# Expert weights of a two-layer mixture: down weights unsplit, the others split by two engines, more load buffers

## The chip, the cores and the metric

The kernel runs on one core of a Trainium2 chip. The core has five engines with their own instruction streams: TensorE (PE, matrix products), VectorE (DVE), ScalarE (ACT), GpSimd (POOL) and SyncE (SP), whose queue issues most of the transfers from DRAM. The metric is the device time in microseconds (us); lower is better. Before the change it is 4615.15 us, the median of three runs (4608.68 to 4620.15).

## The reference, cut to what matters

A first block (differential attention, two gated linear recurrences, an MLP) is followed by two layers. Each layer adds a mixer's output and then a mixture of 16 experts, on 1024 tokens of width 1024, all in float32:

```python
def ec_moe(h, w_router, w_gate, w_up, w_down):
    cap = EC_FACTOR * s // N_EXPERTS                       # 128 tokens an expert
    logits = jnp.einsum('bsd,de->bse', h, w_router)
    aff = jax.nn.softmax(logits, axis=-1)
    gates, idx = lax.top_k(aff.transpose(0, 2, 1), cap)    # each expert takes its own tokens
    xs = jax.vmap(lambda hb, ib: hb[ib])(h, idx)
    g = jnp.einsum('becd,edf->becf', xs, w_gate)           # 1024 -> 512
    u = jnp.einsum('becd,edf->becf', xs, w_up)             # 1024 -> 512
    y = jnp.einsum('becf,efd->becd', jax.nn.silu(g) * u, w_down)   # 512 -> 1024
    y = y * gates[..., None]
    return scatter_add(idx, y)
```

An expert's three matrices have 2 MB each, so a layer reads 16 x 6 MB of expert weights.

## The kernel before, in words

Products of float32 numbers are formed from float32r parts. `split_into` (L98, L99) makes `hi`, the number rounded to float32r by ScalarE, and `lo`, the rest, by a subtraction on VectorE or GpSimd. `mm3` (L91 to L93) then adds three products: hi x hi, hi x lo and lo x hi. A weight chunk of [128, 1024] numbers, 512 KB, is loaded by `whalf` (L114) from SP's queue into a raw buffer and split into a `whi` and a `wlo` buffer; `lo_engine` gives every other subtraction to GpSimd and to VectorE.

A layer's second half is `out_moe`. It first runs the mixer's output projection over eight token tiles (its matrix stands split on chip, in the pool `eT` or `ow`), with the norm and the router's logits of each tile (`moe_in`). While this goes on, the first raw buffers of the pool `mx` are freed one after the other by small GpSimd copies, so that expert weights come in. Then `moe` runs:

- `top_c` finds every expert's 128 best tokens in 15 rounds of comparisons on VectorE and one small product each (L1491);
- `route(e)` builds a one-hot table (L1542), reads out token numbers and gates by small products, and gathers the tokens' rows with an indirect transfer of GpSimd (L1553);
- `tokens` transposes the gathered rows and splits them into `xe`;
- `up(e, ...)` multiplies them with the gate and then the up matrix, four chunks each, into the PSUM tile `pgu`;
- `hidden` takes Silu (L1581) and the product with the up part (L1582), transposes that (L1586) and splits it into `se`;
- `down` multiplies with the four chunks of the down matrix into `pd`;
- `add` scales the result by the gate (L1604) and adds it to the rows in DRAM with an indirect transfer of GpSimd (L1605).

The program's order interleaves experts: the gate and up products of expert e, then the down products of expert e-1. A planner with a cost model sets the final order of each engine's stream from the program's order and the buffers. All twelve chunks of an expert are split, through 18 raw buffers (`mx`) and 8 pairs of hi/lo buffers in the space of the projection's matrix. The first eight chunks of a layer are subtracted by GpSimd alone, while VectorE is at the selection. In layer 1, the last one, `finish` norms the output rows beside the last experts, and gathers, adds and norms the rows of experts 14 and 15 once more at the end (L1980, L1985).

Of the kernel before, what the change touches and what calls it, by code (L numbers as in the profile page):

```python
# [26 lines left out]
class Kern:  # L27
# [6 lines left out]
    # ---------------------------------------------------------------- consts  # L34
# [20 lines left out]
    def exp_ln_table(self):  # L55
        """Exp and Ln from the one table set that holds both."""
        from concourse.act_sets import SETS
        i = [t.name for t in SETS].index("natural_log_exp_and_others")
        self.tc.keep_in_program_order(self.nc.scalar.add_instruction(mybir.InstLoadActFuncSet(
            name=self.nc.get_next_instruction_name(), act_func_set_id=i, ins=[], outs=[])))  # L60

    # ---------------------------------------------------------------- psum
# [3 lines left out]
    def mb(self, name="mb"):  # L66
        """A single bank: the even layer has four of them in place of two pairs."""
# [4 lines left out]
    def pair(self):  # L72
        """Two banks."""
        if self.pss:
            return [self.mb(), self.mb()]
        p = self.mm()
        return [p[:, 0, :], p[:, 1, :]]
# [10 lines left out]
    # ---------------------------------------------------------------- helpers  # L88
# [6 lines left out]
    def split_into(self, src, hi, lo, leng=None):  # L95
        """hi = src rounded to float32r, lo = src - hi, both exact parts of src."""
# [9 lines left out]
    def whalf(self, *srcs, W=None):  # L106
        """Pieces of weights, each [128, n, m], side by side in one 1024-wide chunk (hi, lo)."""
# [13 lines left out]
    def parts(self, w, m, off=0, n=None):  # L121
        """The (hi, lo) pieces of width m of a chunk."""
# [3 lines left out]
    def wsrc(self, w, r0, nk, c0, m):  # L126
        """[128, nk, m] view of the DRAM matrix w: rows r0 + 128 k + p, columns c0..c0+m."""
# [3 lines left out]
    def w128(self, w, c0, W=None):  # L131
        """128 columns of a matrix with 1024 rows: 8 pieces [128, 128]."""
        return self.parts(self.whalf(self.wsrc(w, 0, 8, c0, 128), W=W), 128)

    def w256(self, w, c0, W=None):
        """256 columns of a matrix with 1024 rows: 8 pieces [128, 256]."""
# [5 lines left out]
    def row(self, src, n, name, pool, bufs=None, off=0):  # L142
        """A DRAM vector repeated on every partition."""
# [5 lines left out]
    def colrow(self, cols, out, n):  # L149
        """Columns [128, n] to a row of 128 n values on every partition: out [128, n*128]."""  # L150
# [9 lines left out]
    def rstd(self, ss, n, out):  # L160
        """out = (ss / n + eps) ** -0.5 on a narrow tile."""
# [10 lines left out]
    def ssq(self, xt, out, s):  # L172
        """Sum of squares along the free axis; s: scratch."""
        self.nc.scalar.activation(s, xt, AF.Square, accum_out=out)

    def norm_tile(self, xt, g, pool, xb=2):
        """rms norm of a token tile [128, 1024] with gain row g."""
# [8 lines left out]
    def rstd_dve(self, ss, n, out):  # L186
        """out = (ss / n + eps) ** -0.5 on the vector engine alone: a guess from the bits, three Newton steps."""
# [16 lines left out]
    def norm_tiles(self, xs, g, xn, keep=None):  # L204
        """xn = rms norms of token tiles [128, 1024] with gain row g; rows times keep."""
# [10 lines left out]
    def cols_T(self, xs, hT, t0, g, sh, pool, by_class=False):  # L216
        """Token tiles xs (each [128, 1024]) transposed, times the gain columns g, plus the columns sh,
        into hT (hi, lo) [128, 8, 1024] from token tile t0 on; by_class: token 4 j + c of a tile at
        place 32 c + j."""
# [29 lines left out]
    def norm_T(self, xin, g, hT, sp):  # L249
        """rms norm of the token tiles in DRAM, gain row g, into hT (hi, lo) [128, 8, 1024]."""  # L250
# [11 lines left out]
    def proj_T(self, wl, hT, out, h, k0=0):  # L262
        """out [128 columns, 512 tokens] of half h."""
# [3 lines left out]
    def proj_T2(self, wl, hT, k0=0):  # L267
        """[128 columns, 1024 tokens] in psum."""
# [5 lines left out]
    def proj_N(self, wl, hT, t, out, k0=0):  # L274
        """out [128 tokens of tile t, columns]."""
# [3 lines left out]
    def proj_N2(self, wl, hT, evac, ps, k0=0):  # L279
        """256 columns for all tokens; evac(t2, psum [128, 2 token tiles, 256])."""  # L280
# [6 lines left out]
    # ---------------------------------------------------------------- small vectors and modulation  # L287
    def condition(self, pool):
        """Silu of c, as columns."""
# [9 lines left out]
    def vectors(self, pool):  # L299
        """Small vectors as columns: loaded as rows of 128, transposed at once."""  # L300
# [24 lines left out]
    def ada_sums(self, s, pool, tag, bufs, acc=None):  # L325
        """Section s of the modulation but for its bias, still to be summed over the partitions; acc: what is there."""
# [13 lines left out]
    def ada(self, s, pool, tag, bufs, ps):  # L340
        """Section s of the modulation, as columns mod[:, 8 s : 8 s + 8]."""
# [7 lines left out]
    def mod_cols(self, name, s_sh, s_sc, nm):  # L349
        """Columns g * (1 + scale) and shift for one modulated norm."""  # L350
# [5 lines left out]
    # ---------------------------------------------------------------- attention pieces  # L356
    def q_stack(self, src, pb, dst, scale=1.0):
        """src [64, n] psum at partition pb -> dst [128, n]: float32r head and rest stacked."""
# [6 lines left out]
    def k_stack(self, src, pb, kh, kl, both=True):  # L365
        """src [64, n] psum at partition pb -> kh, kl [128, n]: each part on both halves."""
# [8 lines left out]
    def scores(self, out, q, kh, kl, t):  # L375
        """out [128, 2, 512] = q tile t against all keys, from stacked parts."""
# [8 lines left out]
    def pt_tiles(self, sp, nb):  # L385
        """Transposed weights of two query tiles: [half of the keys][hi, lo] tiles [128 k, 4, 256]."""
# [3 lines left out]
    def p_transpose(self, e, pt, qi, sp=None):  # L390
        """e [128 q, 1024] into pt at query tile qi of the pair; the second half by way of sp and GpSimd."""
# [14 lines left out]
    # ---------------------------------------------------------------- differential attention  # L406
    def branch_a(self, hT, oa, first):
        nc, tc, a = self.nc, self.tc, self.a
        W = a["w_in"]
        with ExitStack() as ctx:  # L410
            sp = ctx.enter_context(tc.tile_pool(name="da", bufs=1))
            self.exp_ln_table()
            # lambda
# [15 lines left out]
            # distances times the head's slope, a quarter of it for the next head  # L429
# [23 lines left out]
    def diff_head(self, sp, Q, KK, V, tab, nlam, ones, gcol, oa, h):  # L453
        nc = self.nc
        for qr in range(4):
            pt = self.pt_tiles(sp, 2)
            rc = sp.tile([128, 2], F32, name="drc", tag="drc", bufs=2)
            for qi in range(2):
# [13 lines left out]
                # (e1 - lam s1 / s2 e2), divided by s1 at the end  # L472
# [22 lines left out]
    def rstd_wide(self, ss, n, out):  # L495
        """out = (ss / n + eps) ** -0.5 over a wide tile."""
# [4 lines left out]
    # ---------------------------------------------------------------- gated linear recurrences  # L501
# [18 lines left out]
    def softplus_neg_abs(self, z, sp, bias=None):  # L520
        """Ln(1 + exp(-|z + bias|))."""
# [1597 lines left out]
```

## Time and profile before

| what | value |
|---|---|
| runs | 4615.15 us median, 4608.68 to 4620.15 (three) |
| profiled execution, first to last instruction | 4606.6 us |
| median run less that span | 8.5 us |
| TensorE busy | 4061.6 us (88%) |
| VectorE, ScalarE, GpSimd busy | 2627.1 (57%), 1967.3 (43%), 1696.7 us (37%) |
| transfers | 514.39 MB, mean 112 GB/s |
| mean granted TensorE clock | 0.917 |

The profiled execution has no time of its own beside its span; the runs' median stands 8.5 us above it. A group's line gives count, busy time, mean duration in ns, the idle time of the engine just before, and what ended that. A timeline's line gives start, duration, engine, source line, operation, output and input, and in brackets an idle time with its releaser. A wait's line gives the total, the count and the longest. TensorE's records overlap, so the time between two starts is what a product costs, not a record's duration.

### The profile page before, as it was taken

The page shows a single profiled execution, that of the slowest core. Times are in us where ns is not written, and L with a number is a line of the kernel's source. Part 1 is how long each engine was busy: PE and PEld are TensorE (multiplying, and loading weights), DVE is VectorE, ACT ScalarE, POOL GpSimd, SP SyncE. Part 2 cuts the span into 40 slices and gives each one's busy share as a digit, 9 for nine tenths or more (in the row PEclk, how much of TensorE's full clock was granted, in tenths as well). Part 3 has the DMA queues.
Part 4 walks back from the last instruction along what each step waited for, and adds up shares of the span by engine and source line. Part 5 has one row for each costly group of instructions (what it writes and reads, how often), then busy time and mean ns, then how long its engine had stood idle before and what let it go on. Part 6 is the DMA issues. An engine that isn't in the chain of part 4 may idle for free. (4 is left out here: it accounts for less than half of the span.)

```text
span 4606.6 us, 57724 instructions
## 1 busy us (share of the span) xinstructions
PE 4061.6 (88%) x21893; PEld 3397.3 (74%) x21893; DVE 2627.1 (57%) x3944; ACT 1967.3 (43%) x3192; POOL 1696.7 (37%) x1082
## 2 busy tenths in 40 slices
PE   6999989899899999998999987778796899986786
PEld 5788867778587888887889866666694787865564
DVE  6545573636434333336255565978638567648886
ACT  3444333432323112114354542556524578734564
POOL 2000031231333212125211222777424467616775
PEclk8999989686999999998989998889897999997898
DMA  4212341021432111122322226788510001066886
GB/s 158 74 49 81 101 132 47 33 84 43 159 119 73 51 42 55 42 60 91 86 72 77 66 74 233 238 278 295 152 43 9 16 19 47 19 224 216 299 292 217
DMA packets 346937, 514.39 MB, mean 112 GB/s; under 512 B 39318, under 2 KB 212769, under 8 KB 346660
## 3 DMA queue, kind: packets, MB, share of 16 engines
q1 hardware_dynamic: 337012, 475.58, 31.8%
q0 software_dynamic: 9648, 35.13, 3.1%
q8 instruction: 172, 2.82, 0.3%
q14 instruction: 105, 0.86, 0.1%
HBM read 418.87 MB, written 83.36 MB: 109 GB/s over the span
## 5 line engine op out<-in xcount | busy, mean ns | idle before, releaser
L99 POOL TENSOR_TENSOR wlo<-wraw,whi 128x1024 fp32r<-128x1024 f32 (+2 forms) x297 | 775.0, 2696 | 1371.9 <-ACT whi L98 1318.2
L98 ACT ACTIVATE whi<-wraw 128x1024 fp32r<-128x1024 f32 (+2 forms) x579 | 597.2, 1041 | 922.4 <-PE mm L92 259.7
L99 DVE TENSOR_TENSOR wlo<-wraw,whi 128x1024 fp32r<-128x1024 f32 (+3 forms) x282 | 651.4, 2323 | 545.7 <-ACT whi L98 513.2
L91 PE MATMUL mm<-h,whi 128*128 128x512 f32 x832 | 331.6, 400 | 8.0 <-DVE xq L649 4.2
L92 PE MATMUL mm<-h,whi 128*128 128x512 f32 x832 | 331.5, 398 | 2.9 <-POOL h L99 1.8
L93 PE MATMUL mm<-h,wlo 128*128 128x512 f32 x832 | 331.5, 399 | 1.4 <-POOL wlo L99 1.1
L91 PE MATMUL pgu<-whi,xe 128*128 128x512 f32 x512 | 216.2, 422 | 10.9 <-ACT xe L98 10.8
L93 PE MATMUL pgu<-whi,xe 128*128 128x512 f32 x512 | 215.9, 422 | 0.0
L912 DVE TENSOR_TENSOR Y<-py,Y 128x1024 f32<-128x1024 f32 x112 | 137.0, 1224 | 133.3 <-PE py L93 133.3
L92 PE MATMUL pgu<-wlo,xe 128*128 128x512 f32 x512 | 212.0, 414 | 0.0
L91 PE MATMUL py<-whi,mr 128*128 128x512 f32 x512 | 201.6, 394 | 9.2 <-DVE mr L921 8.1
L93 PE MATMUL py<-whi,mr 128*128 128x512 f32 x512 | 203.1, 397 | 0.0
L92 PE MATMUL py<-wlo,mr 128*128 128x512 f32 x512 | 202.3, 395 | 0.0
L1023 DVE TENSOR_REDUCE ast<-ps 128x1 f32<-128x1024 f32 x128 | 156.3, 1222 | 66.3 <-PE ps L93 47.6
L91 PEld LDWEIGHTS mm<-h,whi 128*128 128x128 f32 x832 | 156.8, 189 | 47.7 <-issue 5.3
L396 PE MATMUL ptp<-ident,e 128*128 128x128 f32 x1280 | 181.1, 276 | 12.0 <-ACT pf L400 5.1
L92 PEld LDWEIGHTS mm<-h,whi 128*128 128x128 f32 x832 | 157.3, 189 | 41.5 <-POOL h L99 2.3
L93 PEld LDWEIGHTS mm<-h,wlo 128*128 128x128 f32 x832 | 157.2, 189 | 40.6 <-POOL wlo L99 2.0
L91 PE MATMUL pj<-h,whi 128*128 128x512 f32 x384 | 159.7, 416 | 19.1 <-ACT gst L791 18.9
L402 POOL TENSOR_TENSOR pt<-pf,pt 128x512 fp32r<-128x512 f32 x128 | 165.8, 1295 | 10.6
L396 PEld LDWEIGHTS ptp<-ident,e 128*128 128x128 f32 x1280 | 148.3, 142 | 27.2 <-ACT pf L400 11.4
L92 PE MATMUL pd<-wlo,se 128*128 128x512 f32 x256 | 113.4, 443 | 51.6 <-DVE wlo L99 51.6
(636 smaller groups left out, 11488.7 us busy)
## 6 DMA issues: line engine op xcount, KB each, us to landing
wraw<-in_moe_w_gate_dram SPq DMA_DIRECT2D x128, 512.0 KB
wraw<-in_moe_w_up_dram SPq DMA_DIRECT2D x128, 512.0 KB
wraw<-in_moe_w_down_dram SPq DMA_DIRECT2D x128, 512.0 KB
wraw<-in_mlp_w_dram SPq DMA_DIRECT2D x64, 512.0 KB
wraw<-in_w_in_dram SPq DMA_DIRECT2D x52, 512.0 KB
wad<-in_ada_w_dram SPq DMA_DIRECT2D x48, 512.0 KB
gD<-gst SPq DMA_DIRECT2D x24, 512.0 KB
wraw<-x SPq DMA_DIRECT2D x20, 512.0 KB
```

Source lines behind the costliest of these rows:

```text
L91: t.matmul(out, l[0], r[0], start=start, stop=False)
L92: t.matmul(out, l[0], r[1], start=False, stop=False)
L93: return t.matmul(out, l[1], r[0], start=False, stop=stop)
L98: nc.scalar.activation(hi, src, AF.Copy)
L99: (nc.gpsimd if leng == "pool" else nc.vector).tensor_tensor(lo, src, hi.bitcast(F32), op=ALU.subtract)
L396: nc.tensor.transpose(p[:, k, :], e[:, (4 * kg + k) * 128:(4 * kg + k + 1) * 128], self.ident)
L402: nc.gpsimd.tensor_tensor(lo, f, hi.bitcast(F32), op=ALU.subtract)
L912: nc.vector.tensor_tensor(y, pv, y, op=ALU.add)
L1023: nc.vector.tensor_reduce(out=st[:, 0:1], in_=pv, axis=AX.X, op=ALU.min)
```

## The change

It touches the mixtures alone. The pieces, with what is not needed left out:

```diff
+        n = [0]
+        def raw(nm, chunk):
+            pool, bufs = (W[0], W[1]) if n[0] % (W[1] + W[3]) < W[1] else (W[2], W[3])
+            n[0] += 1
+            x = pool.tile([128, 1024], F32, name="wraw", tag="wraw", bufs=bufs)
+            nc.sync.dma_start(x, dap(a[nm], chunk * 128 * 1024, [[1024, 128], [1, 1024]]))
+            return x
+
+        def weights(nm, chunk):
+            x = raw(nm, chunk)
+            hi, lo = [W[2].tile([128, 1024], FR, name=y, tag=y, bufs=W[4]) for y in ("whi", "wlo")]
+            self.split_into(x, hi, lo)
+            return self.parts((hi, lo), 512)
...
-            sT = [sp.tile([128, 4, 128], FR, name="se%d" % j, tag="se%d" % j, bufs=2) for j in range(2)]
+            sT = sp.tile([128, 4, 128], F32, name="se", tag="se", bufs=2)
...
-            self.split_into(p, sT[0], sT[1])
+            nc.scalar.activation(sT, p, AF.Copy)
...
-                w = weights("moe_w_down_2", ((i * 16 + e) * 512 + k * 128) * 1024, [[1024, 128], [1, 1], [1, 1024]])
+                w = raw("moe_w_down_2", (i * 16 + e) * 4 + k)
                 for h in range(2):
-                    self.mm3(p[:, h, :], (sT[0][:, k, :], sT[1][:, k, :]), w[h], k == 0, k == 3)
+                    nc.tensor.matmul(p[:, h, :], sT[:, k, :], w[:, h * 512:(h + 1) * 512], start=k == 0, stop=k == 3)
...
-        slot = self.top_c(lg, sr, cs, begun)
+        slot = self.top_c(lg, sr, cs)
...
-        self.moe(i, xD, hD, lg, opn("mo"), sr, cs, (mx, 18, 8, hl), finish)
+        cls(hl)
+        mw = opn("mw", "left" if side == "right" else "right")
+        self.moe(i, xD, hD, lg, opn("mo", side), sr, cs, (mx, 18, mw, 8, 4), finish)
+        cls("mo", "mr", "mx", "mw")
...
+    for n in ("moe_w_gate_2", "moe_w_up_2"):
+        w = np.asarray(inputs[n]).reshape(2 * 16 * 4, 2, 128, 512)
+        data[n] = np.ascontiguousarray(w.transpose(0, 2, 1, 3))
```

- Down weights and hidden values stay whole: one plain float32 product takes the place of three float32r ones, straight from the raw buffer.
- Gate and up chunks are still split, `hi` by ScalarE and `lo` always by VectorE. GpSimd's part, and the function `begun` that started it, are gone.
- The pool of the projection's matrix is closed and a pool `mw` takes its place, with 8 more raw buffers and 4 pairs in place of 8. Chunks go through the 18 and the 8 raw buffers in turn.
- Gate and up weights are laid out anew before the launch, so that a chunk's two row blocks stand side by side: a partition reads 4 KB in one piece in place of two pieces of 2 KB.
- In layer 1 the pools of `out_moe` lie on the other side of the on-chip memory, where the attention's tiles were.

Comments and function descriptions are taken out as well.

More of the change, by code (lines that the diff above doesn't have):

```diff
@@ L1465, in route_consts, with top_c @@
         return r
-    def top_c(self, aff, sp, cs, begun):
+    def top_c(self, aff, sp, cs):
         nc = self.nc
@@ L1482, in top_c @@
         nc.vector.tensor_copy(ah, at.bitcast(BF)[:, 1::2])
-        begun(at[:, 0:1])
         msk = [ta("msk%d" % i, [128], BF) for i in range(3)]
@@ L1534, in moe @@
                 nc.gpsimd.tensor_tensor(rest[k + 1], rest[k], val[:, :, :, k], op=ALU.subtract)
-        def begun(x):
-            for _ in range(W[2]):
-                nc.gpsimd.tensor_copy(W[3].tile([128, 1024], FR, name="whi", tag="whi", bufs=W[2])[:, 0:1], x)
-        slot = self.top_c(lg, sr, cs, begun)
+        slot = self.top_c(lg, sr, cs)
         def route(e):
@@ L1554, in route @@
             return off, gate, xg
-        def weights(nm, off, dims):
-            self.nw += 1
-            self.lo_engines = ("pool", "dve") if self.nw > W[2] else ("pool",)
-            return self.parts(self.whalf(dap(a[nm], off, dims), W=W), 512)
-        self.nw = 0
+        n = [0]
[10 more added lines that the diff above has]
+            return self.parts((hi, lo), 512)
         def tokens(xg):
@@ L1573, in up @@
             for kg in range(4):
-                wl = weights(nm, ((i * 16 + e) * 1024 + kg * 256) * 512, [[512, 128], [512 * 128, 2], [1, 512]])
+                wl = weights(nm, (i * 16 + e) * 4 + kg)
                 for k in range(2):
@@ L1934, in last @@
             hl = opn("eT", "right")
-            T.extend((self.w_rows("even_w_out_2", hl), hl))
+            T.extend((self.w_rows("even_w_out_2", hl), "eT"))
         self.even_attn(h, a["even_w_in_2"], eD, s1, W2, between, last)
         cls("eb", "ea")
-        self.out_moe(0, *T, eD, 5, x2, x3, h4, opn, cls, banks, None)
-        cls("mo", "mr", "mx", "eT")
+        self.out_moe(0, *T, eD, 5, x2, x3, h4, opn, cls, banks, None, "left")
         dd = opn("dd", "right").tile([128, NT, 768], F32, name="dd")
@@ L1985, in finish @@
                 nc.gpsimd.indirect_dma_start(out=out, out_offset=r[e][0], in_=xn, in_offset=None)
-        self.out_moe(1, wl, hl, cD, 7, x3, x5, h6, opn, cls, banks, finish)
-        cls("mo", "mr", "mx")
-        cls("ow")
+        self.out_moe(1, wl, "ow", cD, 7, x3, x5, h6, opn, cls, banks, finish, "right")
         cls("ps")
@@ L1995, in w_rows, with out_moe @@
                 for k in range(8)]
-    def out_moe(self, i, wl, hl, src, late, xin, xD, hD, opn, cls, banks, finish):
+    def out_moe(self, i, wl, hl, src, late, xin, xD, hD, opn, cls, banks, finish, side):
         nc = self.nc
-        mx = opn("mx")
-        sr = opn("mr")
+        mx = opn("mx", side)
+        sr = opn("mr", side)
         lg = sr.tile([128, NT, 16], F32, name="lg")
         cs = self.route_consts(sr)
-        sp = opn("eo")
+        sp = opn("eo", side)
         half, whole = self.moe_in(i, sp, hD, lg)
```

## The prediction

> **What bounds the kernel now.** I read the page's slices first, then the stages, the groups and waits in them, and single instructions last. A slice is 4606.6 / 40 = 115 us; the two expert mixtures are slices 26 to 29 and 37 to 40.
>
> ```profile
> PE   6999989899899999998999987778796899986786
> POOL 2000031231333212125211222777424467616775
> ```
>
> TensorE is near 9 almost everywhere, but falls to 6 to 8 in the mixtures, just where GpSimd rises. The stages, in the view by window (between the first and the last Silu of a mixture):
>
> ```profile
> core 0: us, PE busy (x) PEld busy (x) DVE busy (x) ACT busy (x) POOL busy (x), PEclk, DMA share, GB/s
> 2915.00:3283.00 368.00, 301.31 (x1319) 238.13 (x1318) 306.34 (x181) 229.61 (x251) 289.31 (x115) 0.90 0.83 274
> 4196.00:4570.00 374.00, 304.16 (x1338) 239.88 (x1336) 314.06 (x196) 233.75 (x260) 288.41 (x114) 0.91 0.82 278
> ```
>
> TensorE idles there for some 70 us a layer, and its granted clock is 0.90. The Silu of an expert (L1581) and the scaling of its share (L1604) mark the experts, in the timeline of ScalarE:
>
> ```profile
> 2915.76 0.60 ACT L1581 ACTIVATE es<-pgu 128x512 f32<-128x512 f32 x1
> 2935.42 1.13 ACT L1604 ACTIVATE whi<-pd,gate 128x1024 f32<-128x1024 f32 x1 [0.28 <-PE pd L93]
> 2953.53 1.12 ACT L1604 ACTIVATE whi<-pd,gate 128x1024 f32<-128x1024 f32 x1 [0.29 <-PE pd L93]
> 3282.32 0.60 ACT L1581 ACTIVATE es<-pgu 128x512 f32<-128x512 f32 x1 [0.28 <-PE pgu L93]
> 4196.49 0.60 ACT L1581 ACTIVATE es<-pgu 128x512 f32<-128x512 f32 x1
> 4570.01 0.58 ACT L1581 ACTIVATE es<-pgu 128x512 f32<-128x512 f32 x1
> ```
>
> Fifteen steps take 366.6 and 373.5 us: 24.4 and 24.9 us an expert. One step, 2935.4 to 2953.5, took 18.1 us: there the split weights were ready and TensorE alone set the pace. So about 6.5 us a step are waits. For what, the groups, two waits and the timeline say:
>
> ```profile
> L99 DVE TENSOR_TENSOR wlo<-wraw,whi 128x1024 fp32r<-128x1024 f32 x97 | 268.9, 2791 | 81.3 <-ACT whi L98 77.5 <-DMA wraw<-in_moe_w_gate_dram 3.8
> L99 POOL TENSOR_TENSOR wlo<-wraw,whi 128x1024 fp32r<-128x1024 f32 x97 | 266.3, 2873 | 70.7 <-ACT whi L98 70.5
> L98 ACT ACTIVATE whi<-wraw 128x1024 fp32r<-128x1024 f32 x194 | 204.0, 1062 | 105.9 <-PE pd L93 46.1 <-PE pgu L93 44.4 <-issue 5.3
> L99 DVE TENSOR_TENSOR wlo<-wraw,whi x282: 410/1272/13774, 30.1 to 4578.9; 128x1024 fp32r<-128x1024 f32 x137, 128x768 fp32r<-128x768 f32 x2, 128x256 fp32r<-128x256 f32 x1, 128x384 fp32r<-128x384 f32 x1
> 3083.77 6.69 POOL L99 TENSOR_TENSOR wlo<-wraw,whi 128x1024 fp32r<-128x1024 f32 x2
> 3084.84 3.41 DVE L99 TENSOR_TENSOR wlo<-wraw,whi 128x1024 fp32r<-128x1024 f32 x1
> 3090.61 1.78 POOL L1553 DMA_INDIRECT wraw<-h,idx  x1 [0.15 <-issue]
> 3091.47 1.21 DVE L99 TENSOR_TENSOR wlo<-wraw,whi 128x1024 fp32r<-128x1024 f32 x1
> PE pd L92 <- DVE wlo L99: 25.8, 5, 5.8
> PE pse L1586 <- DVE xe L99: 19.4, 7, 5.0
> SPq L114 <- POOL wlo L99: 151.7, 46, 32.9
> SPq L114 <- DVE wlo L99: 133.1, 60, 13.8
> ```
>
> The subtraction (L99) takes VectorE 1.21 us when GpSimd runs none, 3.41 us beside one, and up to 13.8 us; its mean here is 2.79. The two engines hinder each other, six chunks each cost both some 17 us a step, and TensorE and the weight loads' queue wait behind them. The bound of the mixtures is the splitting.
>
> **The change, part by part.** Per expert, twelve chunks of 512 KB.
>
> Removed: four of twelve splits, so four L98 (4 x 1.06 us of ScalarE) and four L99. GpSimd keeps its two indirect transfers only. Hidden values need one copy (L98) and no L99.
>
> Moved: the eight remaining L99 all go to VectorE. The price is bounded by 1.21 us (alone) and 2.79 (mean beside GpSimd); I take 1.22, since GpSimd has no tensor work left and the 1.21 us row ran beside an indirect transfer. VectorE also has the one-hot table `oh`, the pieces of `xe`, and the product `es`, whose shape is that of `xe`:
>
> ```profile
> L1542 DVE TENSOR_TENSOR oh<-one_to,slot 128x1024 bf16<-128x1024 bf16 x9 | 22.4, 2487 | 5.3 <-PE pj L1546 5.3
> L99 DVE TENSOR_TENSOR xe<-pxe,xe 128x512 fp32r<-128x512 f32 x26 | 16.8, 676 | 0.0
> ```
>
> Sum: 8 x 1.22 + 2 x 0.68 + 0.68 + at most 2.49 + 0.3 (gate, index) = 14.6 us a step. ScalarE: 8 x 1.06 + three pieces of 0.6, Silu 0.6, L1604 1.1 = 12. Both lie under TensorE.
>
> Added: a float32 product in place of three float32r ones. The trace has none in the mixture; the nearest is the gMLP's, two products in four records, beside the cadence of gate and up:
>
> ```profile
> 2240.59 1.98 PE L1151 MATMUL pm<-z,zwt 128*128 128x512 f32 x4 [0.20 <-DVE zwt L1143]
> L1151 PE MATMUL pm<-z,zwt x8: 592/592/697, 2240.6 to 2245.1; 128*128 128x512 f32 x8
> 4200.17 0.39 PE L91 MATMUL pgu<-whi,xe 128*128 128x512 f32 x1
> 4200.41 0.39 PE L92 MATMUL pgu<-wlo,xe 128*128 128x512 f32 x1
> ```
>
> A float32 record starts every (1.98 - 0.59) / 3 = 0.463 us, so a product is 0.926 us; three float32r are 3 x 0.233 = 0.70. Eight products a step (four chunks, two halves): 8 x (0.926 - 0.70) = +1.8 us on TensorE. Its step becomes 18.1 + 1.8 = 19.9. So TensorE's work grows; it gains only by not waiting.
>
> Buffers: 26 raw in place of 18, hi/lo pairs 4 in place of 8. A pair is in use for 6 x 0.233 = 1.4 us; refilling takes about 0.35 + 1.06 + 0.15 + 1.22 + 0.15 = 2.9 (durations above; the gaps are an estimate from the 0.28 in the L1604 row). Four pairs turn round in 5.6 us, against 4.3, so the loop holds, with 1.3 us of slack for VectorE's other pieces. During the 7.4 us of down products four chunks get ready. What the slack does not take I put at 0.6 us a step (0 to 2, the latter when `oh` and an `xe` fall among the splits). **Step: 20.5 us.** Behind a delayed L98, ScalarE's queue holds the next L98, Silu and `xe`, for which TensorE would wait.
>
> Loads: gate and up rows grow from 2 KB to 4 KB a partition. The rates, first two stretches with mostly 2 KB rows and then 4 KB alone, and two crowded ones in the mixture; and what a mixture moves:
>
> ```profile
> 2832.00:2836.00 4.00, 4.00 (x18) 3.20 (x18) 1.72 (x9) 1.13 (x4) 0.00 (x0) 1.00 1.05 390
> 4560.00:4564.00 4.00, 4.00 (x19) 3.23 (x18) 1.34 (x2) 3.79 (x8) 0.00 (x0) 1.00 1.03 419
> 3180.00:3200.00 20.00, 15.75 (x69) 11.95 (x68) 14.93 (x11) 11.52 (x13) 17.52 (x7) 0.83 1.02 352
> 3200.00:3220.00 20.00, 15.49 (x70) 12.32 (x69) 17.11 (x11) 13.10 (x15) 17.88 (x7) 0.97 0.92 302
> q0 software_dynamic: 4188, 15.23, 16.2%
> ```
>
> Some 28 of 192 chunks are there when the mixture starts, so 164 x 0.524 + 15.2 (indirect) = 101 MB have to come in about 320 us: 316 GB/s. The chip gave 352 under full load with the short rows; I expect about 370 and no wait. That is a margin of a sixth, not more.
>
> Selection of the tokens: the small product of a round (L1491) waited 2.57 us for VectorE beside GpSimd's splits, and 1.40 after them:
>
> ```profile
> 2861.77 0.19 PE L1491 MATMUL po<-cnt,same_expert 128*128 128x4 bf16 x1 [2.57 <-DVE msk L1488]
> 2877.50 0.19 PE L1491 MATMUL po<-cnt,same_expert 128*128 128x4 bf16 x1 [1.40 <-DVE msk L1488]
> ```
>
> Eight slow rounds cost 8 x 1.2 = 9 us more than fast ones; against it stand four first L99 now queued in VectorE among the rounds, 4 x 1.22 = 4.9 us. I take a gain of 3 us a layer (a loss of 3 to a gain of 8).
>
> The pools' sides: in layer 1 the raw buffers now lie where the attention's tiles were, so their first loads, and the router's small ones ahead of them in SP's queue, wait for its end. But SP issues them late already:
>
> ```profile
> 4103.54 2.48 SPq L114 DMA_DIRECT2D wraw<-in_moe_w_gate_dram  x4
> ```
>
> That is 93 us before that layer's first Silu (4196.5), and the output projection covers it: 18 chunks are 9.4 MB, 24 us at 390 GB/s. I put it at nothing; without that cover it would be these 24 us. The eight further buffers open once that projection has read its matrix, and fill during the selection, as eight freed ones did before.
>
> Sum, layer 0: from the first Silu to the end of the last down product (3295.7) 379.9 us now; then 15 x 20.5 + 7.4 (the last down product) + 1.3 (the wait for its hidden values, an estimate) = 316: -64. Layer 1: 373.5 to 307.5: -66; its end hangs on the indirect transfers, not on the splits. The last down product of layer 0, and in layer 1 the scaling of share 13 and the addition of share 15:
>
> ```profile
> 3295.30 0.40 PE L93 MATMUL pd<-whi,se 128*128 128x512 f32 x1
> 4543.38 1.12 ACT L1604 ACTIVATE whi<-pd,gate 128x1024 f32<-128x1024 f32 x1 [0.28 <-PE pd L93]
> 4589.90 1.28 DVE L1980 SCALAR_TENSOR_TENSOR wraw<-pd,gate,wraw 128x1024 f32<-128x1024 f32 x1 [3.56 <-DMA wraw<-x,idx]
> ```
>
> From share 13 to share 15 are 46.5 us now, with a step of some 26 in it; the chain of scatter, eight loads, scatter and gather does not shrink with the step, so I give back 2. Selection: -6. Total -64 - 64 - 6 = -134 us: a span of 4473. The runs' median, 4615.15, is 8.5 us above the profiled span; I keep that: **4481 us**.
>
> **The rivals.** Loads bind. If they only reach 302 GB/s, 101 MB take 335 us, 15 more a layer: 4511; at the mean of the stage, 276, 366 us: 4571. Against it: that mean has the queue waiting 285 us for buffers. Chance 0.10.
>
> Four pairs are too few. A step with 2 us more (22.5) gives 4481 + 2 x 15 x 2 = 4541. For it: ScalarE already waits 46.1 and 44.4 us for TensorE to free pairs, with eight. 0.15.
>
> VectorE becomes the bound, the slower side: were L99 2.79 us even without GpSimd, eight and the rest make 27.1 us a step, 4481 + 30 x 6.6 = 4679. It decides from 8d + 4.8 = 24.7, so d = 2.5 us. The rows of 1.21 and 3.41 speak against it. 0.05. The Trainium skill, SBUF — State Buffer, "Who interferes with whom", has a VectorE instruction with two SBUF inputs fully blocked by a GpSimd one that reads SBUF, and not slowed otherwise. By that rule the price falls back to the 1.21 of the row and the time is the forecast; by the mean it is this rival. The row of 13.8 us agrees with the rule.
>
> Float32 is dearer: four records of 0.463 a product make 12.5 + 14.8 + 0.6 = 27.9 us a step, 4703. Against it: L1151 shows eight records for four products. 0.04. The Trainium skill, FP8 and Floating Point Precision, "TensorE Precision Notes", counts four passes for true float32, which speaks against this edit. Were each pass a record, it would be this rival; by the two records of L1151 a record holds two passes, and the forecast stands.
>
> The change does not act, since another limit keeps the step at 24.7: 4615. The 18.1 us step speaks against it. 0.03.
>
> **How the numbers follow.** The forecast has 0.63, with its own range of 4450 to 4515 (steps of 19.9 to 21.5, selection's bounds). The range 4440 to 4570 takes in the loads and the pairs, and leaves out 0.12 and a little at the low end. No change means within 0.3%, about what runs of this kernel can tell. Faster 0.63 + 0.10 + 0.15 = 0.88, same 0.03, slower 0.09.
>
> **What would show it.** Right: Silus 20 to 21 us apart; VectorE's L99 at 1.2 us; two float32 records a down product, 0.46 us apart; clock near 1.0 in the mixtures; TensorE's waits on L99 gone. Wrong: L99 over 2 us, records over 0.6 us apart, ScalarE or TensorE waiting on each other's pairs for more than 2 us a step, or down products waiting for raw chunks.

## The result, and the profile after

The changed kernel takes 4461.01 us, the median of four runs (4452.69 to 4473.79); the kernel before, beside it, 4617.65 us (4608.68 to 4620.29). The ratio is 0.9669 with a 95% interval of 0.9645 to 0.9693: 156.6 us less. The forecast was 4481 us, 20 us too high.

The profiled run of after took 4473.79 us with a span of 4472.0, so only 1.8 us lie outside the span. The profiled run of before, with a span of 4606.6, was therefore the fastest of its runs (4608.68), and the profiled run of after is the slowest of its four. The spans differ by 134.6 us, the medians by 156.6. Both differences are used below.

The slices of the page of after, with its two groups of interest (columns of a group: busy us, mean ns, idle time before and its releaser):

```profile
PE   6999989989889999998999998699895988996997
POOL 2000021322153212124411121111123646630111
PEclk8999989886899999999998998799996999997998
L99 DVE TENSOR_TENSOR wlo<-wraw,whi 128x1024 fp32r<-128x1024 f32 (+1 forms) x354 | 441.9, 1251 | 632.0 <-ACT whi L98 604.1
L1600 PE MATMUL pd<-wraw,se 128*128 128x512 f32 x512 | 236.6, 596 | 1.9 <-ACT se L1592 1.9
```

In the mixtures (now slices 27 to 29 and 37 to 40) GpSimd has fallen to about 1 and TensorE is at 9 in the slices that lie wholly in a mixture (28, 38 and 39). From the first to the last Silu of each mixture, by window (PE, PEld, DVE, ACT and POOL busy, then granted clock, DMA share, GB/s), and the groups of layer 0's:

```profile
2920.71:3217.72 297.01, 292.65 (x1213) 198.97 (x1212) 182.26 (x193) 168.72 (x189) 39.79 (x26) 1.00 0.93 330
4134.79:4437.09 302.30, 294.32 (x1216) 199.09 (x1214) 187.68 (x210) 177.24 (x204) 41.59 (x27) 1.00 0.93 335
```
```profile
L99 DVE TENSOR_TENSOR wlo<-wraw,whi 128x1024 fp32r<-128x1024 f32 x118 | 144.3, 1225 | 86.5 <-ACT whi L98 85.0 <-DMA wraw<-in_moe_w_gate_dram 0.2 <-DMA wraw<-in_moe_w_down_dram 0.2
L98 ACT ACTIVATE whi<-wraw 128x1024 fp32r<-128x1024 f32 x117 | 123.8, 1061 | 87.5 <-PE pgu L93 87.4
```

TensorE is busy in 98.5% of the first window, at full granted clock (before: 82% and 0.90). The subtraction takes 1.225 us. The arrow has turned: before, TensorE waited for the subtraction; now ScalarE's copies (L98) wait 87.4 us for TensorE to free a pair. TensorE sets the pace. The timeline of ScalarE has the first and last Silu (L1586) of both layers, and scalings of shares (L1609) in layer 0:

```profile
2920.71 0.60 ACT L1586 ACTIVATE es<-pgu 128x512 f32<-128x512 f32 x1
...
2958.43 1.12 ACT L1609 ACTIVATE whi<-pd,gate 128x1024 f32<-128x1024 f32 x1 [1.89 <-PE pd L1600]
2978.03 1.11 ACT L1609 ACTIVATE whi<-pd,gate 128x1024 f32<-128x1024 f32 x1 [1.03 <-PE pd L1600]
...
3157.44 1.12 ACT L1609 ACTIVATE whi<-pd,gate 128x1024 f32<-128x1024 f32 x1 [0.18 <-PE pd L1600]
3178.10 1.12 ACT L1609 ACTIVATE whi<-pd,gate 128x1024 f32<-128x1024 f32 x1 [0.17 <-PE pd L1600]
...
3217.72 0.60 ACT L1586 ACTIVATE es<-pgu 128x512 f32<-128x512 f32 x1 [9.68 <-PE pgu L93]
...
4134.79 0.60 ACT L1586 ACTIVATE es<-pgu 128x512 f32<-128x512 f32 x1
...
4437.09 0.58 ACT L1586 ACTIVATE es<-pgu 128x512 f32<-128x512 f32 x1
```

Fifteen steps take 297.0 and 302.3 us: 19.8 and 20.15 us an expert, in place of 24.4 and 24.9. The first of the fifteen intervals holds only a part of a step (14.9 us), so a whole step is a little longer than the mean. Early steps are mostly 19.6 us, late ones 20.7. In the early ones TensorE shows no idle time. From the tenth step on it stands still at the change of expert, for the token pieces `xe` or for another small piece, 0.53 or 0.82 us in each late step. Two early steps by window, from Silu to Silu, and the first of the waits in TensorE's timeline:

```profile
3035.15:3074.36 39.21, 39.21 (x169) 26.95 (x168) 25.44 (x28) 23.25 (x26) 5.84 (x3) 1.00 1.02 369
```
```profile
3096.47 0.50 PE L91 MATMUL pgu<-whi,xe 128*128 128x512 f32 x1 [0.58 <-ACT xe L98]
```

**The account of the spans.** Each stretch runs from a first record to a last one in both traces. "Projection" is the output projection of a layer's second half.

| stretch | before | after | difference |
|---|---|---|---|
| start to the first router product of layer 0 (L1441) | 2760.7 | 2771.5 | +10.8 |
| from there to the end of layer 0's last down product | 535.0 | 456.7 | -78.3 |
| to the last projection product of layer 1 | 834.0 | 842.3 | +8.3 |
| to the first Silu of layer 1 | 66.8 | 64.3 | -2.5 |
| to the end | 410.1 | 337.2 | -72.9 |
| sum | 4606.6 | 4472.0 | -134.6 |

The first and third rows are work that the change doesn't touch; TensorE's instructions of the first are the same in the same order in both kernels. At 2628 us the two traces stand level; by 2706 us after is 10.5 us behind. The profile shows what differs there: in layer 0's attention the granted clock (the figure before the DMA share) was 0.99 in the run of before and 0.84 in that of after. The first line is of before, the second of after:

```profile
2620.00:2710.00 90.00, 86.13 (x478) 69.81 (x478) 70.74 (x204) 65.17 (x173) 25.11 (x18) 0.99 0.33 97
```
```profile
2620.00:2710.00 90.00, 87.06 (x426) 69.76 (x425) 64.42 (x178) 58.11 (x151) 22.66 (x17) 0.84 0.28 85
```

In the same 90 us TensorE got through 478 products in one run and 426 in the other. Without these 19.1 us the spans would differ by 153.7 us, close to the medians. The third row is settled less well: its clock was lower only in part, but two kernels below that keep the pools as before took 840.0 and 843.5 us for it, so the moved pools don't explain it.

**The selection.** Last product of the projection in layer 0, first and last round; first before, then after, which also shows the first four splits:

```profile
2846.57 0.40 PE L93 MATMUL mb<-whi,wlo 128*128 128x512 f32 x1
2854.91 0.16 PE L1491 MATMUL po<-cnt,same_expert 128*128 128x4 bf16 x1 [1.72 <-DVE msk L1488]
...
2885.43 0.19 PE L1491 MATMUL po<-cnt,same_expert 128*128 128x4 bf16 x1 [1.40 <-DVE msk L1488]
```
```profile
2857.28 0.40 PE L93 MATMUL mb<-whi,wlo 128*128 128x512 f32 x1
2857.71 3.91 ACT L98 ACTIVATE whi<-wraw 128x1024 fp32r<-128x1024 f32 x4 [2.21 <-PE mb L93]
2858.81 4.63 DVE L99 TENSOR_TENSOR wlo<-wraw,whi 128x1024 fp32r<-128x1024 f32 x4 [0.40 <-ACT whi L98]
2869.57 0.16 PE L1490 MATMUL po<-cnt,same_expert 128*128 128x4 bf16 x1 [1.71 <-DVE msk L1487]
...
2891.75 0.19 PE L1490 MATMUL po<-cnt,same_expert 128*128 128x4 bf16 x1 [1.40 <-DVE msk L1487]
```

The rounds shrink from 30.5 to 22.2 us, since no GpSimd subtraction runs beside them. But the first round now comes 12.3 us after the projection, not 8.3: the four first splits stand on ScalarE and VectorE ahead of the last token tile's norm.

### The profile page after: what moved, and what is told of

It reads as the page before. It is cut to its first block, busy times and chain, and to the rows that moved or that the text cites. A ratio compares the mean times of both kernels' runs of the same rounds, so it can differ in the third digit from the quotient of the medians.

```text
span 4472.0 us, 56648 instructions
## 1 busy us (share of the span) xinstructions
PE 4064.7 (91%) x21637; PEld 3331.6 (74%) x21637; DVE 2365.1 (53%) x3984; ACT 1839.8 (41%) x3064; POOL 1140.9 (26%) x866
## 3 DMA queue, kind: packets, MB, share of 16 engines
q8 instruction: 170, 2.79, 0.3%
## 5 line engine op out<-in xcount | busy, mean ns | idle before, releaser
L98 ACT ACTIVATE whi<-wraw 128x1024 fp32r<-128x1024 f32 (+3 forms) x451 | 465.3, 1035 | 926.5 <-PE mm L92 260.9
L99 DVE TENSOR_TENSOR wlo<-wraw,whi 128x1024 fp32r<-128x1024 f32 (+1 forms) x354 | 441.9, 1251 | 632.0 <-ACT whi L98 604.1
L99 POOL TENSOR_TENSOR wlo<-wraw,whi 128x1024 fp32r<-128x1024 f32 (+3 forms) x97 | 229.0, 2361 | 1269.7 <-ACT whi L98 1244.3
L1600 PE MATMUL pd<-wraw,se 128*128 128x512 f32 x512 | 236.6, 596 | 1.9 <-ACT se L1592 1.9
L91 PE MATMUL pgu<-whi,xe 128*128 128x512 f32 x512 | 216.7, 424 | 5.2 <-ACT xe L98 5.2
L93 PE MATMUL pgu<-whi,xe 128*128 128x512 f32 x512 | 204.7, 400 | 0.0
L91 PE MATMUL pj<-h,whi 128*128 128x512 f32 x384 | 159.3, 415 | 16.8 <-ACT gst L791 16.6
```

What stands on the lines that cost most here:

```text
L91: t.matmul(out, l[0], r[0], start=start, stop=False)
L93: return t.matmul(out, l[1], r[0], start=False, stop=stop)
L98: nc.scalar.activation(hi, src, AF.Copy)
L99: (nc.gpsimd if leng == "pool" else nc.vector).tensor_tensor(lo, src, hi.bitcast(F32), op=ALU.subtract)
L1600: nc.tensor.matmul(p[:, h, :], sT[:, k, :], w[:, h * 512:(h + 1) * 512], start=k == 0, stop=k == 3)
```

## The experiments

The theory at this point: the mixture was held by two engines that slow each other, and TensorE takes over once the subtractions run on VectorE alone. The main rival: only the number of splits matters, whoever does them. "Step" is the mean distance of the Silus in layer 0 and layer 1.

| kernel | median us | ratio to before, 95% interval | steps, us |
|---|---|---|---|
| changed | 4461.0 | 0.9669 (0.9645 to 0.9693) | 19.8, 20.15 |
| 1: changed, GpSimd back | 4514.7 | 0.9777 (0.9749 to 0.9805) | 20.85, 21.1 |
| 2: before, VectorE alone | 4484.8 | 0.9726 (0.9698 to 0.9754) | 20.1, 20.25 |
| 3: changed, down weights split | 4475.7 | 0.9688 (0.9661 to 0.9716) | 19.7, 20.1 |
| 4: changed, 2 KB rows | 4466.9 | 0.9660 (0.9637 to 0.9683) | 19.8, 20.2 |
| 5: before, float32 down products | 4481.2 | 0.9700 (0.9672 to 0.9728) | 19.8, 20.5 |
| 6: changed, 18 raw and 8 pairs | 4475.4 | 0.9690 (0.9673 to 0.9708) | 19.6, 20.3 |
| 7: changed, half of the down products | 4435.9 | 0.9612 (0.9586 to 0.9637) | 19.1, 19.0 |
| 8: changed, two of four down chunks split | 4464.1 | 0.9659 (0.9639 to 0.9679) | 19.3, 20.0 |
| 9: run 6 with GpSimd back | 4486.9 | 0.9723 (0.9708 to 0.9738) | 19.7, 20.3 |
| 10: changed, three pairs | 4454.7 | 0.9655 (0.9640 to 0.9670) | 19.7, 20.0 |
| 11: changed, pairs open early | 4459.7 | 0.9668 (0.9654 to 0.9681) | 19.8, 19.95 |
| 12: runs 8 and 11 together | 4447.2 | 0.9636 (0.9623 to 0.9649) | 19.4, 19.7 |

### Which part brought the gain (runs 1, 2, 3 and 5)

**Run 1, GpSimd back.**

```diff
-            self.split_into(x, hi, lo)
+            self.split_into(x, hi, lo, leng=("pool", "dve")[n[0] % 2])
```

> The changed kernel, but every other subtraction of the gate and up weights goes to GpSimd again (4 of 8 an expert). Theory A, the two engines hinder each other: VectorE's 128x1024 L99 goes back from 1.23 us to a mean above 2 us, and with four pairs a chunk takes 1.4 + 0.35 + 1.06 + 0.15 + 2.8 + 0.15 = 5.9 us to turn round, 1.48 us a chunk against the 1.40 that TensorE needs; the step grows from 19.8 to 21 to 22.5 us, 4500 to 4540 us in all. Theory B, the gain came from splitting 8 chunks in place of 12, whoever does it: step 19.8, 4461 within 12 us, since 4 x 2.8 us on either engine lie far under the step.

Measured: 4514.7 us, 54 more than the changed kernel, steps of 20.85 and 21.1 us. The groups of its first mixture:

```profile
L99 POOL TENSOR_TENSOR wlo<-wraw,whi 128x1024 fp32r<-128x1024 f32 x60 | 152.0, 2555 | 95.8 <-ACT whi L98 95.8
L98 ACT ACTIVATE whi<-wraw 128x1024 fp32r<-128x1024 f32 x117 | 123.9, 1060 | 113.7 <-PE pgu L93 104.5 <-issue 9.2
L99 DVE TENSOR_TENSOR wlo<-wraw,whi 128x1024 fp32r<-128x1024 f32 x59 | 116.2, 1975 | 108.8 <-ACT whi L98 108.8
```

VectorE's subtraction is back at 1.98 us on average and GpSimd's takes 2.56. The time is that of theory A, the mean and the step fall just short of it. TensorE's waits in that mixture are 12.1 us for `es`, which stands in VectorE's queue behind a slowed subtraction, and 4.0 us for subtractions themselves. The Trainium skill, SBUF — State Buffer, "Who interferes with whom", says that the two engines contend only where they share a port; these means, and the 1.225 us once GpSimd has no subtraction, agree.

**Run 2, the kernel before with VectorE alone** from a layer's ninth chunk on, and twelve splits an expert:

```diff
-            self.lo_engines = ("pool", "dve") if self.nw > W[2] else ("pool",)
+            self.lo_engines = ("dve",) if self.nw > W[2] else ("pool",)
```

> The kernel before, with all twelve splits and three float32r products a down product, but from the ninth chunk of a layer on every subtraction goes to VectorE. Theory A: GpSimd's part is the whole trouble. VectorE then has 12 x 1.22 + 3 x 0.68 + 0.68 + 2.5 + 0.3 = 20.2 us a step, TensorE 18.1: step 20.2 to 21 in place of 24.7, 4480 to 4505 us, nearly all of the change's gain without the plain float32 products. Theory B: VectorE cannot carry twelve; the fewer splits are needed: step 23 or more, 4565 or more.

Measured: 4484.8 us, 132.6 less than before, the time of theory A. The window of its first mixture:

```profile
2909.26:3210.46 301.20, 280.94 (x1313) 223.81 (x1312) 256.95 (x267) 228.19 (x249) 41.87 (x26) 0.97 0.97 331
```

VectorE is busy for 257 of 301 us and TensorE for 281: twelve splits on one engine fit. But VectorE does not set the pace, as theory A had it: it has 17.1 us of work a step, not 20.2. Steps without a wait of TensorE take 18.5 us, others 21 to 23; its waits, 20.2 us in all, are for the pieces of `xe`, from VectorE and from ScalarE, and for the gates.

**Run 5, the kernel before with float32 down products alone**; every other subtraction stays on GpSimd:

```diff
-                w = weights("moe_w_down_2", ((i * 16 + e) * 512 + k * 128) * 1024, [[1024, 128], [1, 1], [1, 1024]])
+                w = tile()
+                nc.sync.dma_start(w, dap(a["moe_w_down_2"], ((i * 16 + e) * 4 + k) * 128 * 1024, [[1024, 128], [1, 1024]]))
                 for h in range(2):
-                    self.mm3(p[:, h, :], (sT[0][:, k, :], sT[1][:, k, :]), w[h], k == 0, k == 3)
+                    nc.tensor.matmul(p[:, h, :], sT[:, k, :], w[:, h * 512:(h + 1) * 512], start=k == 0, stop=k == 3)
```

> The kernel before with the plain float32 down products alone: 8 splits an expert, every other one on GpSimd, 18 raw buffers, 8 pairs, rows of 2 KB. Theory A (hindering): VectorE's L99 stays above 2 us, but each engine has 4 chunks in place of 6; 8 pairs give slack: step 20.5 to 22.5, 4495 to 4555 us, slower than the changed kernel by 30 or more. Theory B (fewer splits are all): step 19.8 to 20.2, 4460 to 4480.

Measured: 4481.2 us, 136.2 less than before, steps of 19.8 and 20.5. The window and VectorE's group:

```profile
2918.07:3215.55 297.48, 290.23 (x1201) 197.99 (x1200) 190.21 (x135) 164.71 (x185) 205.35 (x83) 0.99 0.97 339
```
```profile
L99 DVE TENSOR_TENSOR wlo<-wraw,whi 128x1024 fp32r<-128x1024 f32 x59 | 157.5, 2677 | 60.3 <-ACT whi L98 59.9
```

This goes half against theory A. By the mean the two engines hinder each other as before (2.68 us against 2.79), yet the steps are nearly those of the changed kernel: with eight splits an expert there is room for it under TensorE. The mean also hides what differs. In the first mixture of before, six subtractions of VectorE last 7.4 to 13.8 us, 71 us together, each beside three or more subtractions of GpSimd in a row; here the longest takes 5.5 us. One of the six in before, what GpSimd did, and TensorE, which waited 4.98 us for it:

```profile
3119.23 13.77 DVE L99 TENSOR_TENSOR wlo<-wraw,whi 128x1024 fp32r<-128x1024 f32 x1
3119.62 12.29 POOL L99 TENSOR_TENSOR wlo<-wraw,whi 128x1024 fp32r<-128x1024 f32 x5
3133.05 0.52 PE L92 MATMUL pd<-wlo,se 128*128 128x512 f32 x1 [4.98 <-DVE wlo L99]
```

Either edit alone takes off the bound and some 85% of the gain; the two don't add.

**Run 3, the changed kernel with the down weights split** (the hidden values too):

```diff
-                w = raw("moe_w_down_2", (i * 16 + e) * 4 + k)
+                w = weights("moe_w_down_2", (i * 16 + e) * 4 + k)
                 for h in range(2):
-                    nc.tensor.matmul(p[:, h, :], sT[:, k, :], w[:, h * 512:(h + 1) * 512], start=k == 0, stop=k == 3)
+                    self.mm3(p[:, h, :], (sT[0][:, k, :], sT[1][:, k, :]), w[h], k == 0, k == 3)
```

> The changed kernel, but the down weights and hidden values are split again, by ScalarE and VectorE, and multiplied as three float32r products. Theory A (VectorE then sets the pace at 20.2 us, TensorE needs only 18.1): step 20.2 to 21.5, 4470 to 4515 us, so the plain float32 products are worth 10 to 50 us. Theory B (TensorE sets the pace in both): the step falls by the 1.8 us that the plain products added, to 18.1 plus about 0.6, and the time to 4405 to 4430.

Measured: 4475.7 us, at the good end of theory A, with steps below its range: VectorE has 17.0 us of work a step, not the 20.2 that it took. The medians put the worth of the plain products at 15 us, but the interval overlaps that of the changed kernel. TensorE is busy for 277.8 of 295.6 us here, VectorE for 254.9: the step of 19.7 us is set by neither alone. Steps without a wait of TensorE take 18.4 us; of its waits, 17.8 us in all, 14.6 are for the pieces of `xe`.

### Buffers and loads (runs 4, 6, 9 and 10)

**Run 4, rows of 2 KB.**

```diff
-            nc.sync.dma_start(x, dap(a[nm], chunk * 128 * 1024, [[1024, 128], [1, 1024]]))
+            nc.sync.dma_start(x.rearrange("p (n m) -> p n m", n=2),
+                              dap(a[nm], chunk * 128 * 1024, [[512, 128], [512 * 128, 2], [1, 512]]))
```

> The changed kernel with the gate and up weights in their old layout: a partition of a chunk comes in two rows of 2 KB again. Its mixtures move 330 and 335 GB/s at a DMA share of 0.93, and 357 to 377 GB/s at a share of 1.00 to 1.03 while buffers are free. Theory A (the loads have margin over the whole mixture): DMA share 0.95 to 1.0, no TensorE wait on raw chunks, step within 0.3 us of 19.8 and 20.15, 4455 to 4470 us. Theory B (loads are close to binding, long rows are needed): at 340 GB/s about 100 MB take 295 us and the last experts wait, 5 to 20 us more a layer, 4470 to 4500 us.

Theory A: 4466.9 us, the same steps, 330 and 335 GB/s as with long rows. The new layout brings nothing that can be measured.

**Run 6, the buffers of before.**

```diff
-        self.moe(i, xD, hD, lg, opn("mo", side), sr, cs, (mx, 18, mw, 8, 4), finish)
+        self.moe(i, xD, hD, lg, opn("mo", side), sr, cs, (mx, 18, mw, 0, 8), finish)
```

> The changed kernel with the buffers of before: 18 raw ones and 8 pairs in place of 26 and 4. Theory A (neither binds in the steady part, but the first splits are queued on ScalarE and VectorE ahead of the last token tile's norm): steps stay at 19.7 to 20.2; with eight first splits in place of four the selection starts 8 x 1.22 - 4 x 1.22 = 5 us later a layer, less what the first step gains by having its pairs ready (up to 4 us), 4460 to 4473 us in all. Theory B (26 raw buffers are needed for the loads): steps of 21 or more, 4490 or more. Theory C (four pairs cost the 1.1 us by which late steps, 20.7, exceed early ones, 19.6): late steps of 19.6, 4440 to 4452 us.

Measured: 4475.4 us, near theory A, with steps of 19.6 and 20.3; late steps stay at 20.7, so theory C falls, and B with it. The selection begins 4.5 us later, as eight first splits now stand ahead of it (last projection product and first round):

```profile
2847.64 0.40 PE L93 MATMUL mb<-whi,wlo 128*128 128x512 f32 x1
2864.47 0.17 PE L1490 MATMUL po<-cnt,same_expert 128*128 128x4 bf16 x1 [1.71 <-DVE msk L1487]
```

That is 16.8 us in place of 12.3. Fewer pairs help by having fewer first splits. Raw buffers and pairs changed together here, and no run changes the sides of the pools alone.

**Run 9, run 6 with the edit of run 1.**

```diff
-            self.split_into(x, hi, lo)
+            self.split_into(x, hi, lo, leng=("pool", "dve")[n[0] % 2])
...
-        self.moe(i, xD, hD, lg, opn("mo", side), sr, cs, (mx, 18, mw, 8, 4), finish)
+        self.moe(i, xD, hD, lg, opn("mo", side), sr, cs, (mx, 18, mw, 0, 8), finish)
```

> The changed kernel with 18 raw buffers and 8 pairs, and every other subtraction on GpSimd: the run with GpSimd back, but with eight pairs in place of four. That run had steps of 20.9 and 21.1 us, the one with eight pairs on VectorE alone 19.6 and 20.3. Theory A (GpSimd's slower subtractions cost time only because four pairs turn round too slowly): steps 19.6 to 20.4, 4465 to 4490 us, with VectorE's L99 mean again above 1.9 us. Theory B (the hindering itself costs): steps near 21, 4500 to 4525 us.

Measured: 4486.9 us. VectorE's group in its first mixture:

```profile
L99 DVE TENSOR_TENSOR wlo<-wraw,whi 128x1024 fp32r<-128x1024 f32 x57 | 125.3, 2202 | 59.1 <-ACT whi L98 58.6
```

Its mean is 2.20 us, but the steps are 19.7 and 20.3, those of run 6: theory A. Of TensorE's 12.1 us of waits for `es` in run 1 only 0.7 are left. So run 1 lost time in its steps because it had four pairs for slow subtractions, which then start late and stand ahead of `es` (run 9 also has fewer raw buffers, which gained nothing in run 6). Of the 11 us that run 9 loses against run 6, some 8 lie ahead of the first expert: its first round comes 21.0 us after the projection, 4.1 later than in run 6, in both layers.

**Run 10, three pairs.**

```diff
-        self.moe(i, xD, hD, lg, opn("mo", side), sr, cs, (mx, 18, mw, 8, 4), finish)
+        self.moe(i, xD, hD, lg, opn("mo", side), sr, cs, (mx, 18, mw, 8, 3), finish)
```

> The changed kernel with three pairs of hi/lo buffers in place of four. Theory A, the turn-round of 5.6 us (1.4 in use, 0.35 + 1.06 + 0.15 + 1.22 + 0.15 to refill) holds: 5.6 / 3 = 1.87 us a chunk against the 1.40 that TensorE takes, 8 chunks x 0.47 = 3.7 us a step, of which the down products, which need no pair and stand in two or three blocks, give back up to half: step 21.6 to 23.5, 4515 to 4570 us. Theory B, pairs have slack beyond what was worked out: step within 0.5 us of 19.8, 4455 to 4475 us.

Measured: 4454.7 us, theory B. The expectation had a slip: 5.6 us is what four pairs offer (4 x 1.4), and a chunk needs 4.33. Three pairs offer 4.2, which is just enough:

```profile
2911.88:3207.40 295.52, 294.38 (x1216) 198.16 (x1214) 180.22 (x194) 168.07 (x192) 37.83 (x27) 1.00 0.92 333
```

TensorE is busy 99.6% of the time, and most of the steps are 19.7 to 19.9 us long: the planner put the small pieces otherwise, and the waits of the late steps are gone. That could not be foreseen from buffer counts. Its runs overlap those of the changed kernel.

### What would come next (runs 7, 8, 11 and 12)

**Run 7, half of the down products.**

```diff
-                for h in range(2):
-                    nc.tensor.matmul(p[:, h, :], sT[:, k, :], w[:, h * 512:(h + 1) * 512], start=k == 0, stop=k == 3)
+                for h in range(2 if k < 2 else 0):
+                    nc.tensor.matmul(p[:, h, :], sT[:, k, :], w[:, h * 512:(h + 1) * 512], start=k == 0, stop=k == 1)
```

> The changed kernel with the down products of two of the four blocks left out (all four chunks are still loaded), so the shares are incomplete. TensorE has 8 x 0.463 = 3.7 us less a step. Theory A (TensorE alone sets the step): step 16.1, 4461 - 30 x 3.7 = 4350 us. Theory B (the loads stand close behind): about 100 MB at 375 GB/s take 267 us a layer in place of 297, so only some 30 us a layer are gained: step about 17.8, 4400 us, with TensorE or the splits waiting on raw chunks.

Both theories fall: 4435.9 us and steps of 19 us. Two early steps take 16.6 and 15.7, then most are 18 to 22. No wait on raw chunks shows. TensorE's timeline at a change of expert:

```profile
2994.74 1.08 PE L1572 MATMUL pxe<-ident,wraw 128*128 128x128 f32 x8
2996.81 0.50 PE L91 MATMUL pgu<-whi,xe 128*128 128x512 f32 x1 [0.98 <-ACT xe L98]
2997.15 0.40 PE L92 MATMUL pgu<-wlo,xe 128*128 128x512 f32 x1
2999.17 1.12 PE L1591 MATMUL pse<-ident,es 128*128 128x128 f32 x4 [1.62 <-DVE xe L99]
...
3000.94 0.63 PE L92 MATMUL pgu<-wlo,xe 128*128 128x512 f32 x1
3001.36 0.63 PE L93 MATMUL pgu<-whi,xe 128*128 128x512 f32 x1
3001.79 0.63 PE L91 MATMUL pgu<-whi,xe 128*128 128x512 f32 x1
...
3003.68 0.40 PE L92 MATMUL pgu<-wlo,xe 128*128 128x512 f32 x1
3003.92 0.40 PE L93 MATMUL pgu<-whi,xe 128*128 128x512 f32 x1
```

The next expert's pieces `xe` stand in ScalarE's queue behind a Silu and a copy of a split, and in VectorE's behind a one-hot table, `es` and a subtraction, and TensorE waits 0.98 and 1.62 us for them. For some 2.6 us after that its products start 0.43 us apart, not 0.23, at a granted clock of 0.53: six of them cost 1.2 us more. Together that is 3.8 us, all of the 3.7 that this step was to save. Over the first mixture the waits for `xe` come to 27.6 us, 1.8 a step; the slow stretch follows in some steps only, and a step with the same two waits and no slow stretch took 19.3 us. The Trainium skill, TensorE: Matmul & The Clock Gate, "Part 1: The HAM clock gate", has TensorE fall to half its clock after an idle window of about 3.4 us; the spacing and the 0.53 agree with the half, but the two waits are shorter than that window, and no run here shows its length.

**Run 8, two of four down chunks split**, with the hidden values as float32r pieces for these two and whole for the others.

```diff
-                w = raw("moe_w_down_2", (i * 16 + e) * 4 + k)
+                w = (weights if k < 2 else raw)("moe_w_down_2", (i * 16 + e) * 4 + k)
                 for h in range(2):
-                    nc.tensor.matmul(p[:, h, :], sT[:, k, :], w[:, h * 512:(h + 1) * 512], start=k == 0, stop=k == 3)
+                    if k < 2:
+                        self.mm3(p[:, h, :], (sT[1][:, k, :], sT[2][:, k, :]), w[h], k == 0, False)
+                    else:
+                        nc.tensor.matmul(p[:, h, :], sT[0][:, k, :], w[:, h * 512:(h + 1) * 512], start=False, stop=k == 3)
```

> The changed kernel with two of an expert's four down chunks split again (ScalarE and VectorE) and the other two plain float32. TensorE saves 4 x (0.926 - 0.70) = 0.9 us a step; VectorE goes from 12.4 busy (185 in 297 us a layer) to about 15.2 us, ScalarE from 11.4 to 13.6. Theory A (TensorE sets the step): 18.9 in place of 19.8, 4461 - 30 x 0.9 = 4434 us. Theory B (more splits bring back waits for pieces in VectorE's queue, as in the run with all down weights split, whose steps went from 18.4 to 23): step 19.6 to 20.2, 4455 to 4475 us.

Measured: 4464.1 us, the time of theory B, with steps of 19.3 and 20.0 between the two. TensorE has less work, but waits more for small pieces (8.7 us in the first mixture, 4.4 in the changed kernel); the total doesn't move.

**Run 11, the pairs open early.** The four pairs lie in the pool that is open during the projection; the freeing copies of the projection and the last rows' tiles follow suit. Of the raw buffers, 10 lie there and 16 in `mw`.

```diff
-            hi, lo = [W[2].tile([128, 1024], FR, name=y, tag=y, bufs=W[4]) for y in ("whi", "wlo")]
+            hi, lo = [W[0].tile([128, 1024], FR, name=y, tag=y, bufs=W[4]) for y in ("whi", "wlo")]
...
-        self.moe(i, xD, hD, lg, opn("mo", side), sr, cs, (mx, 18, mw, 8, 4), finish)
+        self.moe(i, xD, hD, lg, opn("mo", side), sr, cs, (mx, 10, mw, 16, 4), finish)
```

> The changed kernel with the four pairs in the pool that is open during the projection (10 raw buffers and the pairs there, 16 raw ones in the space of the projection's matrix), so that the first four chunks can be split before the last token tile is normed. Theory A (the four first L99, 4.6 us together, stand ahead of that norm and delay the selection): from the last product of the projection to the first round of the selection 8.3 us in place of 12.3, 4 us a layer, 4449 to 4456 us. Theory B (the early splits only move into the way of another tile's norm, or fewer chunks are there at the start): no gain, 4458 to 4470 us.

Measured: 4459.7 us, in theory B's range. Two of the first subtractions (the other two stand just before), the last projection product and the first round, from the timeline:

```profile
2810.35 2.35 DVE L99 TENSOR_TENSOR wlo<-wraw,whi 128x1024 fp32r<-128x1024 f32 x2
2848.61 0.40 PE L93 MATMUL mb<-whi,wlo 128*128 128x512 f32 x1
2856.94 0.16 PE L1490 MATMUL po<-cnt,same_expert 128*128 128x4 bf16 x1 [1.71 <-DVE msk L1487]
```

The splits move into the projection, and the first round comes 8.3 us after it, as theory A says to the tenth (8.7 in layer 1). The mechanism is shown by the trace; a gain of 8 us in all is not shown by the runs (4454 to 4468 us).

**Run 12** joins the diffs of runs 8 and 11.

> As the run with the early pairs, and two of the four down chunks split: steps of 19.3 and 20.0 us as in the run that had that alone, and the selection 4 us earlier a layer. If both hold: 4461 - 8 - 2 to 8 = 4445 to 4452 us. If four pairs for ten chunks or the moved buffers take it back: 4458 to 4470 us.

Measured: 4447.2 us, and each of its five runs (4446.2 to 4451.6) is below each of the four of the changed kernel. It is the fastest of all that compute everything, some 14 us or 0.3% below the changed kernel and 7.5 us below run 10; its interval still overlaps that of the changed kernel.

## Why the prediction was right, and where it was off

**The bound.** Right that the mixtures were held by the splitting, with two engines hindering each other. It left open that either half of the change is nearly enough: runs 2 and 5. And it worked with the mean of 2.79 us, where a few subtractions of up to 13.8 us made TensorE wait longest for them.

**The price of a subtraction**, 1.22 us, was measured at 1.225. VectorE's whole sum, 14.6 us a step, came out at 12.2, mainly because `oh` takes 1.22 us without GpSimd, not 2.49; this changes nothing, as both lie under TensorE. The rivals with 2.79 us, with dearer float32 and with no effect are gone.

**The step**: 20.5 forecast, 19.8 and 20.15 measured. This is the part of the sum that was off, in three terms. A float32 product was put at 2 x 0.463 us, from four records of the gMLP. In the mixture (the timeline of after) it is less:

```profile
3103.45 2.74 PE L1600 MATMUL pd<-wraw,se 128*128 128x512 f32 x6
3105.62 0.80 PE L91 MATMUL pgu<-whi,xe 128*128 128x512 f32 x1
3106.26 2.74 PE L1600 MATMUL pd<-wraw,se 128*128 128x512 f32 x6
3108.43 0.80 PE L92 MATMUL pgu<-wlo,xe 128*128 128x512 f32 x1
3109.06 0.40 PE L93 MATMUL pgu<-whi,xe 128*128 128x512 f32 x1
```

Twelve records and two float32r products take 5.61 us: (5.61 - 2 x 0.233) / 12 = 0.43 us a record, 0.86 a product, and 8 x (0.86 - 0.70) = 1.3 us a step in place of 1.8. The 18.1 us that the sum starts from were too little, by some 0.3: that interval, from share to share, shows only 2 of the 8 small products with the one-hot table, and in run 3, which multiplies as before, TensorE's steps without a wait take 18.4. So a step without stalls is 19.6, as the window of after shows, and not the forecast 19.9: two errors that in part cancel. The stalls are nothing in the early steps and about 1.1 us in the late ones, 0.4 to 0.5 on average, where 0.6 was put. The difference of the means, some 0.5 us over 30 steps, is 15 of the 20 us.

**Four pairs** were forecast to hold, with 1.3 us of slack. Run 10 shows that even three hold. **The loads** were forecast not to bind: 330 and 335 GB/s, no TensorE wait on a chunk. The rate of 370 was reached in the full stretches, but run 4 shows that the longer rows weren't needed.

**The selection** was put at -3 us a layer, between +3 and -8. From the first router product to the first Silu of layer 0 it is 155.0 against 149.2 us, -5.8. The 8 us of faster rounds came as worked out, and the four first splits took about 4 back; but they don't stand among the rounds, as was forecast, but ahead of the last norm. In layer 1 it is -2.5 from the end of the projection.

**The 8.5 us** between span and median weren't a fixed part but the distance of one run from the others; the fixed part is about 2. The forecast span of 4473 against 4472.0 is luck: 19.1 us more in stages that weren't touched hide as much less in the mixtures.

## What to carry to other kernels

Where two edits each lift the same bound, don't add their gains: runs 2 and 5 each have most of it. Work out the step that the next engine allows, here TensorE's 19.6 us, but add what it waits for small pieces in other engines' queues: in run 2, with VectorE busy for 85% of the time and ScalarE for 76%, steps were 20.1 us where TensorE alone needs 18.5. Look at the longest instructions of a group and not only at their mean. Buffers that are too few show only when what refills them is slow, so price the refill against what the consumer takes; and look at what the first fills stand ahead of. Compare two profiled runs stage by stage, with the untouched stages first: they tell how much of a difference is not the change's.

## What was not expected of the hardware

Between runs, the first router product of layer 0, with the same TensorE work ahead of it, came between 2755.5 us (run 2) and 2777.6 us (run 1). Where this was followed up, from 2620 to 2710 us, the granted clock was 0.84 in the run of after against 0.99 in that of before; in run 1 it was 0.81, in run 2 1.00. A spread of 22 us is more than several of the differences studied here. The two stalls of run 7, 2.6 us together, cost another 1.2 us, because the products behind them started 0.43 us apart in place of 0.23, at a granted clock of 0.53. And in before a VectorE subtraction beside GpSimd's was not merely slower: one took 13.77 us and ended 1.1 us after the last of five GpSimd subtractions in a row, where one alone takes 1.21.
